# Weight parts stored with the columns of two neighbouring tiles by turns, and other start offsets for the activations

## Chip, cores and metric

The kernel runs on one core of one Trainium2 chip. The metric is the device time of one execution in microseconds (us); lower is better. The shapes are fixed: 256 positions, width 1024, two layers, feed-forward width 2816.

## What is computed

Both layers have the same frame, and the mixer in the middle differs: layer 0 has a convolution mixer, layer 1 attention.

```python
for layer in range(DEPTH):                                   # DEPTH = 2, SEQ = 256, D_MODEL = 1024
    x = x + 0.5 * swiglu_ffn(rms_norm(x, ffn1_norm[layer]), ffn1_w_gate_up[layer], ffn1_w_down[layer])
    h = rms_norm(x, mix_norm[layer])
    if layer % 2 == 0:
        x = x + conv_mixers(h, ...)          # projection 1024 -> 2560, two causal convolutions, projection back
    else:
        x = x + dilated_attention(h, ...)    # 16 heads of 64, projection 1024 -> 3072 and back
    x = x + 0.5 * swiglu_ffn(rms_norm(x, ffn2_norm[layer]), ffn2_w_gate_up[layer], ffn2_w_down[layer])
return rms_norm(x, final_norm)
```

Here `swiglu_ffn` is `(silu(x @ gate) * (x @ up)) @ w_down`, with 1024 to 2 x 2816 and back.

## The kernel before

The weights come as a stream of units. A unit is 128 partitions by 2048 float32: 16 tiles of 128 x 128, side by side, 1 MB, fetched by one DMA (`load`, into one of four buffers `raw`). Activations are held transposed, features on the partitions and the 256 positions along the row, so a weight tile is the stationary operand of a matmul and the activations are the moving operand.

Most units are split in two by `split(u)`: ScalarE copies `raw` to `w1` with rounding to the short type that TensorE takes in one pass (`F32R`, L127), and VectorE stores the rest, `w2 = raw - w1` (L128). Both work on halves of 1024 columns (some early units on quarters of 512). `w1` and `w2` have four buffers each, so a split waits until TensorE has finished with the unit four places earlier. Five units (`whole`) are not split and are multiplied as plain float32 (L161).

The activations are split in the same way into two parts, next to each other in the row: `xs` (inputs of a projection) and `gs` (the inner activations of a feed-forward). Three forms of product follow. `mm2` (L169, L170) multiplies `w1` with both activation parts in one matmul of 512 columns and then `w2` with the first part, 256 columns: this is "a pair" below. `mm3` (L163 to L165) does the same work as three matmuls of 256 columns, with `w1` loaded twice. For the values of the attention (L164 and so on with 512 columns) the roles are swapped: the activations are stationary and the weights are moving. Every matmul loads its stationary operand anew; the load of the next one runs while the present one streams.

The stages follow each other in time: in a feed-forward, 22 units of gate and up (`project2`, or `project` with `mm3` for a few of them), then 176 tiles of down (`mm2`, the last output tile with `mm3`). There are four feed-forwards, a convolution mixer between the first two and an attention between the last two. [...]

Where things lie in a row of the on-chip memory is set by hand. A first tile named "gap" fills up to a multiple of `LINE` = 1024 bytes, so that the weight buffers start on such a multiple; each weight tile is 512 bytes long. `XS_START` gives, for each norm and layer, how many bytes behind the start of its memory `xs` begins, and `GS_START` the same for `gs` of the four feed-forwards.

Of the kernel before, what the change touches and what calls it, by code (L numbers as in the profile page):

```python
# [10 lines left out]
F32 = mybir.dt.float32  # L11
# [6 lines left out]
P = 128  # L18
# [15 lines left out]
UT = 16  # L34
# [25 lines left out]
WIDEC = 0  # L60
LINE = 1024
BASE = 16512
XS_START = {"F1": (256, 32), "MX": (192, 256), "F2": (256, 32)}
GS_START = (800, 0, 800, 736)
GROUPS = ((0, 2), (2, 4), (4, 6), (6, 8))
M_POOL = [0, 0, 0, 0]
T_POOL = [0, 0, 0, 0]
# [27 lines left out]
def trunk(ctx: ExitStack, tc: tile.TileContext, xin, wst, cst, bia, idn, out):  # L95
    nc = tc.nc
# [12 lines left out]
    raw, w1, w2 = {}, {}, {}  # L109
# [8 lines left out]
    def split(u):  # L118
        if u in whole:
            return  # L120
        w1[u] = w1s.tile([P, UT * P], F32R, name="w1")
        w2[u] = w2s.tile([P, UT * P], F32R, name="w2")
        n = max(2, PIECES.get(u, 1), FINE.get(u - first_conv, 1))
        h = UT * P // n
        for i in range(n):
            c = slice(i * h, (i + 1) * h)
            nc.scalar.copy(w1[u][:, c], raw[u][:, c])  # L127
            nc.vector.tensor_sub(w2[u][:, c], raw[u][:, c], w1[u][:, c].bitcast(F32))  # L128
        del raw[u]

    def advance(u, ahead_split=ahead_split):
        while at["load"] < min(n_units, u + ahead_load):
            load(at["load"])
            at["load"] += 1
        while at["split"] < min(n_units, u + ahead_split):
            split(at["split"])
            at["split"] += 1


    first_conv = NF + NF * ND // UT  # L140
    whole = {0} | {first_conv + i for i in WHOLE} | {first_conv + 10, first_conv + 11}

    class Stream:
        def __init__(self, u):
# [2 lines left out]
        def tile(self, t, n=1):  # L147
            u, s = self.u + t // UT, t % UT
            c = slice(s * P, (s + n) * P)
            return (raw[u][:, c],) if u in whole else (w1[u][:, c], w2[u][:, c])  # L150

    used = [0]

    def take(n):
        st = Stream(used[0])
        used[0] += n
        return st
# [207 lines left out]
    def ffn(norm, after, between=None, first=None):  # L365
        _, r = norm.end(True, first is None)
        with tc.tile_pool(name="gp", bufs=1, reuse_waits="tile") as gp:
            st = take(NF)
            start = GS_START[st.u // FFN_STEP] // 4
            gs = gp.tile([P, NF * 2 * S + start], F32R, name="gs")[:, start:].rearrange(  # L370
# [339 lines left out]
    for lo, hi in START:  # L710
        c = slice(2 * lo * P, 2 * hi * P)
# [5 lines left out]
    for _ in range(WARM):  # L717
        nc.tensor.matmul(cold, ones, ones, start=True, stop=True)
    norm = Norm(C_F1, start=XS_START["F1"][0])
    for layer in range(DEPTH):  # L720
        nxt = Norm(C_MX + layer * ND, start=XS_START["MX"][layer])
        if layer == 0:
            ffn_first(norm, nxt)
        else:
            ffn(norm, nxt)
        norm, nxt = nxt, Norm(C_F2 + layer * ND, start=XS_START["F2"][layer])
        (conv if layer % 2 == 0 else attention)(norm, nxt)
        if layer < DEPTH - 1:
            norm, nxt = nxt, Norm(C_F1 + (layer + 1) * ND, start=XS_START["F1"][layer + 1])
            ffn(norm, nxt)  # L730
            norm = nxt
    with tc.tile_pool(name="fp", bufs=1, reuse_waits="tile") as fp:
# [6 lines left out]
        _, r = rsqrt_of([last.sums, last.sq], D, RMS_EPS, eps)  # L739
        for i, (lo, hi) in enumerate(GROUPS):  # L740
            n = hi - lo
# [93 lines left out]
```

## Time and profile before

| | |
|---|---|
| median of 3 runs | 969.8 us (968.5 to 969.87) |
| the profiled execution | 970.47 us, of which span 968.7 us |
| TensorE matmul / weight load busy | 953.3 us (98%) / 854.3 us (88%) |
| VectorE / ScalarE / GpSimd busy | 738.5 us (76%) / 557.8 us (58%) / 47.9 us (5%) |
| instructions; DMA | 15285; 176.27 MB, mean 182 GB/s |
| mean granted TensorE clock | 0.993 |

PE is TensorE's matmul row, PEld its weight loads, DVE is VectorE, ACT is ScalarE, POOL is GpSimd. A matmul's record is longer than its share of the time, because matmuls overlap in the pipeline. The pace, the distance from one start to the next, is therefore read from the first and the last start of a long row of equal instructions and their count. [...]

### The profile page before, as it was taken

To read this page: it belongs to the slowest core of one execution; us is meant where nothing else is said; L and a number is where in the kernel's file an instruction comes from. 1 tells how busy PE (TensorE), PEld (TensorE's weight loads), DVE (VectorE), ACT (ScalarE), POOL (GpSimd) and SP (SyncE) were. 2 spreads that over 40 slices of the span, in tenths; PEclk is the share of its full clock that TensorE was granted. 3 is DMA by queue.
4 is the path that set the end of the run, shared out by engine and by line. 5 is a ranking of instruction groups with operands and counts; after the bars stand their busy time and mean duration, and the time that the engine had idled before them with its cause. 6 is when DMAs were issued, how large, how long until landed. Compare 5 with 4: busy or idle time off the path is not lost.

```text
span 968.7 us, 15285 instructions
## 1 busy us (share of the span) xinstructions
PE 953.3 (98%) x5876; PEld 854.3 (88%) x5876; DVE 738.5 (76%) x1401; ACT 557.8 (58%) x1019; POOL 47.9 (5%) x61
## 2 busy tenths in 40 slices
PE   8999999999899999999999999999999999999996
PEld 8988898999798888988988889898888998889886
DVE  7977776688999878766787877666799798778552
ACT  6666554488366566544456565444677566565540
POOL 0000000039600000000000000000000000000000
PEclk9999999999899999999999999999999999999998
DMA  8855555444165555555455555555553455555501
GB/s 329 286 190 201 174 189 203 174 157 149 44 261 180 211 198 194 181 198 187 174 182 210 174 193 200 179 205 202 183 190 129 134 177 211 181 209 176 195 24 44
DMA packets 27289, 176.27 MB, mean 182 GB/s; under 512 B 3024, under 2 KB 3792, under 8 KB 6864
## 3 DMA queue, kind: packets, MB, share of 16 engines
q1 hardware_dynamic: 26784, 174.67, 51.7%
q8 instruction: 46, 0.75, 0.3%
q10 hardware_dynamic: 432, 0.63, 0.2%
q14 instruction: 27, 0.22, 0.1%
HBM read 174.23 MB, written 1.05 MB: 181 GB/s over the span
## 4 chain that ended last, share of the span: by engine, by line
PE 92%; DVE 3%; ACT 2%; POOL 1%; issue 1%; DMA 1%; SPq 0%; DVEq 0%; POOLq 0%; ACTq 0%
PE pa L169 33%; PE pa L170 17%; PE pb L169 15%; PE pb L170 8%; PE pa L165 4%; PE pa L163 4%; PE pa L164 4%; PE pa L161 2%; ACT prod L486 1%; DVE pb L464 1%; PE pb L164 1%; PE pb L163 1%; PE pb L165 1%; POOL yp L487 1%; DVE w L128 1%
## 5 line engine op out<-in xcount | busy, mean ns | idle before, releaser
L169 PE MATMUL pa<-xs,w 128*128 128x512 f32 x1376 | 480.8, 394 | 0.0
L128 DVE TENSOR_TENSOR w<-raw,w 128x1024 fp32r<-128x1024 f32 (+1 forms) x322 | 381.2, 1195 | 126.8 <-ACT w L127 126.1
L127 ACT CAST w<-raw 128x1024 fp32r<-128x1024 f32 (+1 forms) x322 | 325.0, 1027 | 132.5 <-PE pa L169 50.5
L170 PE MATMUL pa<-xs,w 128*128 128x256 f32 x1376 | 385.7, 280 | 0.0
L169 PEld LDWEIGHTS pa<-xs,w 128*128 128x128 f32 x1376 | 258.3, 188 | 58.0 <-DVE xs L191 0.5
L170 PEld LDWEIGHTS pa<-xs,w 128*128 128x128 f32 x1376 | 259.6, 189 | 0.1
L169 PE MATMUL pb<-gs,w 128*128 128x512 f32 x616 | 214.8, 392 | 0.0
L170 PE MATMUL pb<-gs,w 128*128 128x256 f32 x616 | 173.5, 282 | 0.0
L169 PEld LDWEIGHTS pb<-gs,w 128*128 128x128 f32 x616 | 115.7, 188 | 25.2
L170 PEld LDWEIGHTS pb<-gs,w 128*128 128x128 f32 x616 | 116.4, 189 | 0.0
L386 ACT ACTIVATE sl<-v 128x256 f32<-128x256 f32 x88 | 36.8, 419 | 106.3 <-DVE v L341 101.3
L339 ACT COPY sq<-pa 128x256 f32<-128x256 f32 x172 | 63.3, 369 | 30.4 <-PE pa L170 25.1
L164 PE MATMUL pa<-xs,w 128*128 128x256 f32 x272 | 76.5, 282 | 0.1
L163 PE MATMUL pa<-xs,w 128*128 128x256 f32 x272 | 76.5, 283 | 0.0
L165 PE MATMUL pa<-xs,w 128*128 128x256 f32 x272 | 76.4, 281 | 0.0
L340 DVE TENSOR_TENSOR v<-pa,sq 128x256 f32<-128x256 f32 x156 | 64.9, 416 | 0.0
L405 DVE SCALAR_TENSOR_TENSOR x<-pb,x 128x256 f32<-128x256 f32 x60 | 25.3, 422 | 43.0 <-PE pb L170 29.1
L487 POOL TENSOR_TENSOR yp<-yp,prod 128x256 f32<-128x256 f32 x55 | 46.2, 843 | 211.3 <-ACT prod L486 207.3
L190 ACT ACTIVATE xs<-x,const 128x256 fp32r<-128x256 f32 x48 | 24.2, 505 | 56.5 <-DVE x L405 43.2
L341 DVE TENSOR_TENSOR v<-v,rr 128x512 f32<-128x512 f32 x78 | 53.2, 683 | 0.0
L164 PEld LDWEIGHTS pa<-xs,w 128*128 128x128 f32 x272 | 51.8, 190 | 0.5 <-DVE xs L191 0.3
L165 PEld LDWEIGHTS pa<-xs,w 128*128 128x128 f32 x272 | 51.4, 189 | 0.4 <-DVE w L128 0.4
(176 smaller groups left out, 980.8 us busy)
## 6 DMA issues: line engine op xcount, KB each, us to landing
raw<-wst SPq DMA_DIRECT2D x159, 1024.0 KB, 4.8
bt<-bia SPq DMA_DIRECT2D x8, 384.0 KB, 3.3
raw<-wst SPq DMA_DIRECT2D x7, 256.0 KB, 6.3
raw<-wst SPq DMA_DIRECT2D x2, 512.0 KB, 5.6
x<-xin SPq DMA_DIRECT2D x3, 256.0 KB, 6.1
out<-y SPq DMA_DIRECT2D x2, 256.0 KB, 2.5
out<-y ACTq DMA_DIRECT2D x2, 256.0 KB, 2.4
x<-xin SPq DMA_DIRECT2D x2, 128.0 KB, 2.9
```

The source lines that it names most:

```text
L127: nc.scalar.copy(w1[u][:, c], raw[u][:, c])
L128: nc.vector.tensor_sub(w2[u][:, c], raw[u][:, c], w1[u][:, c].bitcast(F32))
L163: nc.tensor.matmul(o, a[0], b[0], start=start, stop=False, skip_group_check=check)
L164: nc.tensor.matmul(o, a[0], b[1], start=False, stop=False, skip_group_check=check)
L165: nc.tensor.matmul(o, a[1], b[0], start=False, stop=stop, skip_group_check=check)
L169: nc.tensor.matmul(o, w[0], b, start=start, stop=False, skip_group_check=True)
L170: nc.tensor.matmul(o[:, 0], w[1], b[:, 0], start=False, stop=stop, skip_group_check=True)
L339: nc.scalar.copy(h, bank[:, 1])
L340: nc.vector.tensor_add(v[:, i], bank[:, 0], h)
L341: nc.vector.tensor_mul(v, v, twice(r))
L386: nc.scalar.activation(sl, v[:, 0], AF.Silu)
L487: nc.gpsimd.tensor_add(yp[:, c], yp[:, c], t)
```

## The change

The two parts of a split unit are stored in another order. Two neighbouring tiles share 256 columns, and their columns alternate: column 0 of the even tile, column 0 of the odd tile, column 1 of the even tile, and so on. `split` reads `raw` as before and writes `w1` and `w2` with a step of two elements (8 bytes); VectorE reads `w1` back with that step. A stationary operand is then 128 elements with a step of two, over 1024 bytes instead of 512. The four units of attention values, whose weights are the moving operand, stay as they were (`plain`), and so do the five `whole` units. The number of instructions and of elements in each is unchanged.

Besides, `XS_START` and `GS_START` get other values: the two entries of the mixers stay, the other four of the first list change, and so do three of the four of the second.

```diff
-XS_START = {"F1": (256, 32), "MX": (192, 256), "F2": (256, 32)}
-GS_START = (800, 0, 800, 736)
+TWIN = 2
+XS_START = {"F1": (32, 128), "MX": (192, 256), "F2": (192, 64)}
+GS_START = (800, 896, 768, 864)
...
         n = max(2, PIECES.get(u, 1), FINE.get(u - first_conv, 1))
-        h = UT * P // n
+        h = UT // TWIN // n
+        r, o1, o2 = raw[u], w1[u], w2[u]
+        if u not in plain:
+            o1, o2 = woven(o1), woven(o2)
+            r = r.rearrange("p (b i c) -> p b i c", i=TWIN, c=P)
+        else:
+            h *= TWIN * P
         for i in range(n):
             c = slice(i * h, (i + 1) * h)
-            nc.scalar.copy(w1[u][:, c], raw[u][:, c])
-            nc.vector.tensor_sub(w2[u][:, c], raw[u][:, c], w1[u][:, c].bitcast(F32))
+            nc.scalar.copy(o1[:, c], r[:, c])
+            nc.vector.tensor_sub(o2[:, c], r[:, c], o1[:, c].bitcast(F32))
...
+    def woven(w):
+
+        return w.rearrange("p (b c i) -> p b i c", i=TWIN, c=P)
...
+    first_values = 3 * first_conv + 14
+    plain = set(range(first_values, first_values + 4))
...
-            return (raw[u][:, c],) if u in whole else (w1[u][:, c], w2[u][:, c])
+            if u in whole:
+                return (raw[u][:, c],)
+            if u in plain:
+                return w1[u][:, c], w2[u][:, c]
+            return tuple(woven(w)[:, s // TWIN, s % TWIN] for w in (w1[u], w2[u]))
```

## Rows read from the trace of the kernel before

**Rows 1.** Page, busy time of each engine, and engines of the chain that ended last.

```profile
PE 953.3 (98%) x5876; PEld 854.3 (88%) x5876; DVE 738.5 (76%) x1401; ACT 557.8 (58%) x1019; POOL 47.9 (5%) x61
...
PE 92%; DVE 3%; ACT 2%; POOL 1%; issue 1%; DMA 1%; SPq 0%; DVEq 0%; POOLq 0%; ACTq 0%
```

**Rows 2.** Longest waits of PE: us in total, times, longest us.

```profile
PE pa L161 <- DVE ya L539: 3.7, 1, 3.7
PE pa L353 <- DMA raw<-wst: 1.8, 1, 1.8
```

**Rows 3.** Busy time by stage: gate-up, down, convolution (second part), attention; columns as headed.

```profile
core 0: us, PE busy (x) PEld busy (x) DVE busy (x) ACT busy (x) POOL busy (x), PEclk, DMA share, GB/s
...
249.00:297.00 48.00, 44.29 (x247) 39.38 (x246) 44.01 (x111) 24.15 (x47) 9.57 (x13) 0.93 0.47 176
...
474.00:597.00 123.00, 123.00 (x726) 109.41 (x725) 100.48 (x176) 73.69 (x131) 0.00 (x0) 1.00 0.54 187
597.00:658.00 61.00, 61.00 (x376) 54.94 (x375) 38.37 (x54) 28.46 (x40) 0.00 (x0) 1.00 0.56 193
658.00:760.00 102.00, 101.89 (x646) 89.25 (x645) 82.04 (x240) 70.76 (x181) 0.00 (x0) 1.00 0.51 173
```

**Rows 4.** One line's matmuls, L170: count, min/median/max ns, first and last start us.

```profile
L170 PE MATMUL pa<-xs,w x171: 277/281/284, 59.7 to 119.8; 128*128 128x256 f32 x171
...
L170 PE MATMUL pa<-xs,w x174: 274/277/280, 309.8 to 369.8; 128*128 128x256 f32 x174
...
L170 PE MATMUL pb<-gs,w x151: 277/281/284, 413.0 to 466.0; 128*128 128x256 f32 x151
...
L170 PE MATMUL pb<-gs,w x145: 282/282/282, 600.0 to 649.9; 128*128 128x256 f32 x145
```

**Rows 5.** The same for L164, one of each three matmuls of `mm3`, four stretches.

```profile
L164 PE MATMUL pa<-xs,w x34: 283/283/283, 19.8 to 31.7; 128*128 128x256 f32 x34
...
L164 PE MATMUL pa<-xs,w x16: 276/276/367, 201.7 to 206.8; 128*128 128x256 f32 x16
...
L164 PE MATMUL pa<-xs,w x77: 281/281/281, 220.1 to 246.9; 128*128 128x256 f32 x77
...
L164 PE MATMUL pb<-gs,w x22: 277/279/280, 950.5 to 957.8; 128*128 128x256 f32 x22
```

**Rows 6.** Float32 units, L161: fifteen merged in the timeline (start, us), and one's durations.

```profile
208.81 3.40 PE L161 MATMUL pa<-xg,raw 128*128 128x256 f32 x15
...
L161 PE MATMUL pa<-xg,raw x64: 377/379/382, 207.7 to 255.3; 128*128 128x256 f32 x64
```

**Rows 7.** Groups by form, the two instructions of a split: busy us, mean ns, idle before.

```profile
L127 ACT CAST w<-raw 128x1024 fp32r<-128x1024 f32 x306 | 316.2, 1049 | 129.1 <-PE pa L169 50.5 <-issue 35.4 <-PE pb L169 24.0
...
L128 DVE TENSOR_TENSOR w<-raw,w 128x1024 fp32r<-128x1024 f32 x306 | 370.0, 1220 | 126.8 <-ACT w L127 126.1
```

**Rows 8.** Timeline of DVE over one gate-up unit: start, us, instruction, idle before.

```profile
520.11 1.22 DVE L128 TENSOR_TENSOR w<-raw,w 128x1024 fp32r<-128x1024 f32 x1 [1.01 <-ACT w L127]
...
521.92 1.21 DVE L128 TENSOR_TENSOR w<-raw,w 128x1024 fp32r<-128x1024 f32 x1
...
524.22 0.43 DVE L388 TENSOR_TENSOR g<-sl,v 128x256 f32<-128x256 f32 x1 [0.15 <-ACT sl L386]
525.66 1.22 DVE L128 TENSOR_TENSOR w<-raw,w 128x1024 fp32r<-128x1024 f32 x1 [1.01 <-ACT w L127]
```

**Rows 9.** Groups by form, two DVE operations of one kind on two SBUF inputs.

```profile
L191 DVE SCALAR_TENSOR_TENSOR xs<-x,const,xs 128x256 fp32r<-128x256 f32 x48 | 23.1, 481 | 12.3 <-ACT xs L190 12.3
...
L527 DVE SCALAR_TENSOR_TENSOR ya<-m,const,ya 128x256 f32<-128x256 f32 x8 | 5.4, 677 | 4.3 <-ACT ya L518 4.3
```

## The prediction

> **What bounds the kernel now.** First the busy shares and the chain that ended last [rows 1]: PE has 98% of the span and 92% of the chain, everything else together 8%. Then PE's waits [rows 2]: the two longest are 3.7 and 1.8 us, so PE is fed nearly all the time. Then the busy time by stage [rows 3]: PE is at 100% in gate-up, down and attention, and only the second part of the convolution shows DVE at 44.0 us of 48 with PE at 44.3. So the time is the number of matmuls times their pace, except in the convolution, where DVE and POOL set the speed and a quicker PE brings little.
>
> The pace is next. In two long stretches a pair (512 and 256 columns) starts every 347 ns: 49.9 us over 144 steps, and 60.0 over 173; in two others every 353 ns: 34.9 over 99 and 60.1 over 170 [rows 4]. The instructions are the same in all four, and the granted clock is 1.00. In the first gate-up stage `xs` begins at byte 256, in the second down stage `gs` begins at 0; these are the slow ones. Yet the stretch from 309.8 us also has `xs` at 256 and is a fast one, so the start sets what paces are possible and not alone which. The matmuls of `mm3` tell the same: a step of three takes 11.9 us over 33, 5.1 over 15, 26.8 over 76 and 7.3 over 21 [rows 5], that is 120, 113, 118 and 116 ns for each 256 columns.
>
> What would it cost without a disturbance? [...] The float32 matmuls of L161 show the fixed cost: fifteen fill 3.40 us with the last one's record of 379 ns [rows 6], so 14 steps take 3.02 us, 216 ns a step, with a weight load behind each. [...] A pair at that rate would take 325 ns, a matmul of 256 columns 109. The pairs lose 22 to 28 ns, the others 4 to 11.
>
> My reading is this. The loss depends on where the moving operand lies, so the two streams that TensorE reads, moving operand and next weights, meet in the memory. A float32 moving operand advances one column in 216/256 = 0.84 ns. A weight load of 128 columns fits in the 113 ns of rows 5's quickest stretch, so at most 0.88 ns a column; taking it to fill that time, it runs at the pace of the float32 operand, and these two, side by side, lose nothing. An `F32R` operand runs at 0.42 to 0.47 ns a column, twice as fast, so it passes the weights' addresses again and again. With a step of two the weights advance 8 bytes a column, as fast as that operand: the streams keep their distance, as in L161. This is inferred, as no row shows a step of two on any engine.
>
> **The change part by part.** *Stationary operands.* A pair goes from 346.7 to 325 ns (21.7 saved) or from 353.3 (28.3 saved). Counts by the loops: gate-up has 17, 21, 21 and 19 units with pairs, 16 each, of which 272 in the slow first stage and 976 elsewhere; down has 154 a stage, one stage slow; queries and keys have 128. Slow: (272 + 154) x 28.3 = 12.1 us. Fast: (976 + 462 + 128) x 21.7 = 34.0 us. Matmuls of 256 columns: 432 in gate-up, 264 in down, 288 in the two output projections. Those where `xs` or `gs` starts at 256 or 0, and the output projections, I put at 120 ns: 192 + 48 + 66 + 288 = 594 x 10.8 = 6.4 us. The other 390 x 7.5 = 2.9 us. The 384 of the convolution's input projection I count at nothing, since DVE hides them; if they counted, it would be 3.2 us. Sum 55.4 us.
>
> What is left over is unknown. The three mm3 paces of 113, 117 and 120 ns lie about 3.3 ns apart, which I take as the price of one meeting. Bounds for the 4968 counted matmuls: none keeps one (0) or each keeps one (16.5 us). I take a quarter, 4.1 us, near the low end, as L161 keeps none.
>
> *Start offsets.* Alone, they would bring the slow stages to the fast pace: 426 x 6.7 + (192 + 48 + 66) x 3.3 = 3.9 us. This lies within the sum above.
>
> *The split.* The instructions and their elements stay, 306 of 1024 columns on each engine [rows 7], but their writes, and one of DVE's reads, get a step of two. No row has such a step. Lower bound 0: nothing in a step saves work. Upper bound from the nearest row, however far: two operations of one kind on 256 columns take 481 and 677 ns [rows 9]; the slower one reads from a shifted place while POOL is busy. That is 0.77 ns a column, or 0.78 us for 1024. I take 0, since a step of 8 bytes is nearer to a dense row than to anything else the trace shows, and keep the upper end for a rival. What hides a smaller cost: in a gate-up unit of 5.55 us (520.11 to 525.66) DVE stands idle 1.01 + 0.15 = 1.16 us [rows 8]. A pace of 325 ns makes the unit 5.20 us, which leaves 0.81 us for two splits. DVE may thus lose 0.40 us on each before the gain shrinks, and 0.58 before the kernel gets slower. ACT has 123 - 74 = 49 us free in that gate-up stage [rows 3], and 0.78 x 44 = 34 us would fit.
>
> [...]
>
> **Rivals.** *A, the streams keep their distance:* 970.5 - 55.4 + 4.1 = 919.2 us in the profiled execution. The median is 0.7 below that execution, so 918.5, rounded 918; with the residue at its bounds and the convolution's 3.2 us, 911 to 931.
>
> *B, only part of the meetings goes,* as the weights may not advance exactly as fast as assumed. Half of 55 us is 28: 942, with 931 to 955 as its range. For it: the unexplained two paces at one start.
>
> *C, the step does nothing and only the offsets count:* 969.8 - 3.9 = 966. Against it: nothing direct.
>
> *D, no change at all.* [...] The trace speaks against it, with 347 against 353 ns for the same pairs at different places, unless something else than the weights causes that.
>
> *E, slower: DVE becomes the bound in gate-up.* At the upper end of 0.78 us for a split, a unit takes 5.55 - 1.16 + 1.56 = 5.95 us, 0.40 more than now, and 88 units give 35 us. The convolution, where DVE is already full, adds some 10 units x 2 x 0.78 = 16 us. Down, with DVE at 38.4 of 61 us [rows 3], has room for 22 x 0.78 = 17 us and still gains its 13 + 3 us, and the output projections 3. So 970 + 35 + 16 - 19 = 1002; it decides from 0.58 us more per split.
>
> [...]
>
> *F, slower: the weight loads suffer.* A load now spans twice as many bytes. If each stretch of bytes it touches meets the moving operand once, the loss above the floor doubles instead of vanishing: 970 + 55 + 3 = 1028. The place is PE, in every pair, and it shows as a pair pace above 353 ns.
>
> **How the numbers follow.** A 0.57, B 0.13, C 0.06, D 0.05, E 0.12, F 0.07. The forecast is A's 918. For 8 in 10 the range takes in A, B, C and D: 910 to 972, leaving out E, F and a little of A. About 0.2% (2 us) is what a measurement of this kernel can tell from no change. Faster: A, B and C, 0.76. Same: D, 0.05. Slower: E and F, 0.19.
>
> **What would show it.** A: L170 paces of 325 to 331 ns in every gate-up and down stage whatever the start, 109 to 113 ns for mm3, the same L127 and L128 means, and DVE's share in gate-up near 90%. B: paces of 332 to 342. C or D: 346 to 347 everywhere, or the old mixture. E: L128 well above 1.6 us and PE waiting in gate-up for DVE. F: paces above 353 with L128 unchanged. The second part of the convolution should stay near 48 us in all of them but E. My sum is wrong first of all if weights do not advance at half the pace of an `F32R` operand.

## The result and the profile after

The changed kernel takes 983.0 us (median of 4 runs, 982.8 to 984.2) against 969.6 for the kernel before: a ratio of 1.0143, with a 95% interval of 1.0125 to 1.0161. It is slower by 13 us (1.4%); the forecast was 918.

The profiled execution has a span of 981.1 us, 12.4 more than before. The page's busy times come first (columns as in [rows 1]).

```profile
PE 966.2 (98%) x5876; PEld 872.6 (89%) x5876; DVE 739.7 (75%) x1401; ACT 584.9 (60%) x1019; POOL 48.0 (5%) x61
```

Then the longest of PE's waits, as in [rows 2].

```profile
PE pa L179 <- DVE ya L557: 3.1, 1, 3.1
```

DVE's total has hardly moved (738.5 before), ACT's has grown by 27 us, and PE does not wait more than before. PE itself has 13 us more, and its weight loads 18 us more. So the loss lies in the pace of PE, and these rows, the counterparts of [rows 4] and [rows 5], show where. Each has the count and the first and last start of the 256-column matmul of the pairs (L188, before L170), in the order of the stages; the last row is one of three of `mm3` (L182, before L164) in the convolution.

```profile
L188 PE MATMUL pa<-xs,w x171: 283/283/283, 59.8 to 119.9; 128*128 128x256 f32 x171
...
L188 PE MATMUL pb<-gs,w x150: 283/283/283, 135.9 to 188.5; 128*128 128x256 f32 x150
...
L188 PE MATMUL pa<-xs,w x172: 278/281/281, 309.9 to 369.9; 128*128 128x256 f32 x172
...
L188 PE MATMUL pb<-gs,w x150: 280/280/281, 415.0 to 468.0; 128*128 128x256 f32 x150
...
L188 PE MATMUL pa<-xs,w x314: 280/280/281, 485.0 to 596.3; 128*128 128x256 f32 x157
...
L188 PE MATMUL pb<-gs,w x142: 278/281/281, 604.9 to 654.7; 128*128 128x256 f32 x142
...
L188 PE MATMUL pa<-xs,w x298: 282/282/282, 795.1 to 902.0; 128*128 128x256 f32 x149
...
L188 PE MATMUL pb<-gs,w x146: 279/279/283, 910.9 to 961.8; 128*128 128x256 f32 x146
...
L182 PE MATMUL pa<-xs,w x90: 283/283/283, 217.9 to 250.0; 128*128 128x256 f32 x90
```

Four stages of before are not among [rows 4]; these are the first down, third gate-up, fourth gate-up and fourth down stage.

```profile
L170 PE MATMUL pb<-gs,w x152: 282/282/282, 134.7 to 187.1; 128*128 128x256 f32 x152
...
L170 PE MATMUL pa<-xs,w x318: 282/282/282, 481.0 to 590.9; 128*128 128x256 f32 x159
...
L170 PE MATMUL pa<-xs,w x303: 279/282/282, 786.5 to 891.2; 128*128 128x256 f32 x152
...
L170 PE MATMUL pb<-gs,w x146: 282/282/282, 900.0 to 950.2; 128*128 128x256 f32 x146
```

The distance from the first to the last start, over the count less one, is the pace of a pair. The starts are given to 0.1 us, so a pace is good to about 1 ns.

| stage | pairs | before, ns | after, ns | more, us |
|---|---|---|---|---|
| first gate-up | 272 | 353 | 353 | 0 |
| first down | 154 | 347 | 353 | 0.9 |
| second gate-up | 336 | 347 | 351 | 1.3 |
| second down | 154 | 353 | 356 | 0.5 |
| third gate-up | 336 | 347 | 356 | 3.0 |
| third down | 154 | 347 | 353 | 0.9 |
| fourth gate-up | 304 | 347 | 360 | 4.0 |
| fourth down | 154 | 347 | 351 | 0.6 |

That is 11 of the 12.4 us. `mm3` pays too: in the convolution's input projection it went from 118 to 32.1/89/3 = 120 ns, about 1 us over its 384 matmuls. Against that stands the convolution's second part, which took 48.0 us before [rows 3] and 46.5 in this execution (columns as in [rows 3]):

```profile
251.60:298.10 46.50, 42.97 (x251) 38.05 (x250) 43.75 (x111) 25.40 (x48) 9.14 (x13) 1.00 0.50 181
```

Before, PE stood still there for 3.7 us, waiting for DVE [rows 2], and behind that wait the granted clock was 0.50 from 261 to 265 us. Here the wait was 3.1 us and the clock stayed at 1.00. The other three executions of the changed kernel have a mean clock of 0.994 or 0.995, near the 0.993 of before, so this belongs to the one execution and not, as far as is known, to the change.

No stage of pairs became faster. The paces spread from 351 to 360 ns, so the place may still count.

The weight loads tell what is new in them. First a stepped load of the kernel after (L187), then a load of the same kernel whose stationary operand stayed dense (the attention's values), each with min/median/max ns.

```profile
L187 PEld LDWEIGHTS pa<-xs,w x1376: 193/197/198, 32.2 to 902.7; 128*128 128x128 f32 x197
...
L182 PEld LDWEIGHTS pa<-w,xs x32: 187/188/192, 664.5 to 686.7; 128*128 128x128 f32 x32
```

197 ns for a load with the step, 188 without. Last the two instructions of a split, by form, as in [rows 7]: ScalarE's copy takes 1144 for 1049 ns, VectorE's subtraction 1223 for 1220.

```profile
L135 DVE TENSOR_TENSOR w<-raw,w 128x1024 fp32r<-128x1024 f32 x306 | 370.7, 1223 | 140.0 <-ACT w L134 139.8
...
L134 ACT CAST w<-raw 128x1024 fp32r<-128x1024 f32 x306 | 344.8, 1144 | 129.6 <-PE pa L187 52.3 <-issue 34.8 <-PE pb L187 23.7
```

### The profile page after: what moved, and what is told of

The parts are those of the page before. It is cut to its first block, busy times and chain, and to the rows that moved or that the text cites. A ratio compares the mean times of both kernels' runs of the same rounds, so it can differ in the third digit from the quotient of the medians.

```text
span 981.1 us, 15285 instructions
## 1 busy us (share of the span) xinstructions
PE 966.2 (98%) x5876; PEld 872.6 (89%) x5876; DVE 739.7 (75%) x1401; ACT 584.9 (60%) x1019; POOL 48.0 (5%) x61
## 4 chain that ended last, share of the span: by engine, by line
PE 90%; DVE 4%; ACT 3%; POOL 1%; issue 1%; DMA 1%; SPq 0%; POOLq 0%; DVEq 0%; ACTq 0%
PE pa L187 33%; PE pa L188 17%; PE pb L187 15%; PE pb L188 7%; PE pa L181 4%; PE pa L183 4%; PE pa L182 4%; ACT prod L504 2%; PE pa L179 1%; PE pb L182 1%; PE pb L181 1%; PE pb L183 1%; DVE pb L482 1%; DVE w L135 1%; POOL yp L505 1%; ACT w L134 1%
## 5 line engine op out<-in xcount | busy, mean ns | idle before, releaser
L187 PE MATMUL pa<-xs,w 128*128 128x512 f32 x1376 | 489.5, 399 | 0.0
L134 ACT CAST w<-raw 128x1024 fp32r<-128x1024 f32 (+1 forms) x322 | 354.2, 1120 | 133.2 <-PE pa L187 52.3
L188 PE MATMUL pa<-xs,w 128*128 128x256 f32 x1376 | 386.6, 281 | 0.0
L187 PEld LDWEIGHTS pa<-xs,w 128*128 128x128 f32 x1376 | 270.5, 197 | 54.0 <-DVE xs L209 0.6
L188 PEld LDWEIGHTS pa<-xs,w 128*128 128x128 f32 x1376 | 270.7, 197 | 0.1
L187 PE MATMUL pb<-gs,w 128*128 128x512 f32 x616 | 217.8, 398 | 0.0
L188 PE MATMUL pb<-gs,w 128*128 128x256 f32 x616 | 173.0, 281 | 0.0
L187 PEld LDWEIGHTS pb<-gs,w 128*128 128x128 f32 x616 | 120.9, 196 | 23.6
L188 PEld LDWEIGHTS pb<-gs,w 128*128 128x128 f32 x616 | 121.1, 197 | 0.0
L182 PE MATMUL pa<-xs,w 128*128 128x256 f32 x272 | 77.2, 284 | 0.1
L183 PEld LDWEIGHTS pa<-xs,w 128*128 128x128 f32 x272 | 53.2, 195 | 0.4 <-DVE w L135 0.2
L182 PEld LDWEIGHTS pa<-xs,w 128*128 128x128 f32 x272 | 53.0, 195 | 0.4 <-DVE xs L209 0.3
```

The costliest lines, as they stand in the source:

```text
L134: nc.scalar.copy(o1[:, c], r[:, c])
L182: nc.tensor.matmul(o, a[0], b[1], start=False, stop=False, skip_group_check=check)
L183: nc.tensor.matmul(o, a[1], b[0], start=False, stop=stop, skip_group_check=check)
L187: nc.tensor.matmul(o, w[0], b, start=start, stop=False, skip_group_check=True)
L188: nc.tensor.matmul(o[:, 0], w[1], b[:, 0], start=False, stop=stop, skip_group_check=True)
```

## The experiments

Four suspects stood after this: the step in TensorE's reading, the step in the writes (ScalarE is slower by 27 us in all, and its stores could disturb TensorE), the new offsets, and a sum of them.

### Step alone

The changed kernel with the offsets of before:

```diff
-XS_START = {"F1": (32, 128), "MX": (192, 256), "F2": (192, 64)}
-GS_START = (800, 896, 768, 864)
+XS_START = {"F1": (256, 32), "MX": (192, 256), "F2": (256, 32)}
+GS_START = (800, 0, 800, 736)
```

> The step of two as in the change, but all start offsets as before. If the stationary operand's step is the cause, most of the 13 us stay: 978 to 986 us, with pair paces above 350 ns in the stages that had 347 before. If the new offsets are the cause, the time falls back to 968 to 972 us with the old paces. ScalarE's split copy should be 1144 ns as in the changed kernel either way.

Measured: 980.75 us, ratio 1.0121 (1.0106 to 1.0136). The step is the larger part. Two rows of L188, at starts that ran at 347 ns before (32 in the third gate-up, 800 in the third down):

```profile
L188 PE MATMUL pa<-xs,w x312: 283/283/283, 484.8 to 594.7; 128*128 128x256 f32 x156
...
L188 PE MATMUL pb<-gs,w x142: 283/283/283, 605.0 to 654.8; 128*128 128x256 f32 x142
```

109.9/311 and 49.8/141 are both 353 ns. At the offsets of before, the step brings every feed-forward stage to 353 ns, the longer of the two old paces, and leaves the stages that had it where they were.

### Offsets alone

The kernel before with the new offsets (the same two lines, the other way round).

> The new start offsets with the old dense layout. If the offsets are the cause, about 980 us. If the step is the cause: 966 to 972 us; places 32, 128, 192, 64 and 800, 896, 768, 864 then show which offset gives which pace with dense weights, those at 0 modulo 128 (128, 896, 768) the slow 353 ns and the others 347.

Measured: 973.2 us, ratio 1.0038 (1.0025 to 1.0051): slower, not the 966 to 972 expected. 32, 864 and 800 gave 347 ns. 128, 896 and 768 were slow as foreseen (351 to 353), but so were 192 and 64, which are 64 modulo 128. The rows of L170, first gate-up (`xs` at 32) and second (192), show 60.0/173 = 347 and 60.1/170 = 353 ns:

```profile
L170 PE MATMUL pa<-xs,w x174: 282/282/282, 59.8 to 119.8; 128*128 128x256 f32 x174
...
L170 PE MATMUL pa<-xs,w x171: 281/281/281, 309.7 to 369.8; 128*128 128x256 f32 x171
```

So with the dense layout the starts at 32 and 96 modulo 128 gave 347 ns here, those at 0 and 64 gave 351 to 353, and the new list has more of the latter than the old. It is no strict rule: the second gate-up stage of the kernel before ran at 347 ns with `xs` at 256.

### Stepped writes, dense reads

```diff
-            return tuple(woven(w)[:, s // TWIN, s % TWIN] for w in (w1[u], w2[u]))
+            return w1[u][:, c], w2[u][:, c]
```

> Old offsets; the split writes with the step of two, but TensorE reads its stationary operands dense, so the weights are in the wrong places and the values differ from the reference. If TensorE's own reading is the cause, 968 to 971 us and the old paces. If ScalarE's longer copy (1144 for 1049 ns) or its stepped writes disturb TensorE, 975 to 985 us.

Measured: 970.7 us, ratio 1.0015 (1.0005 to 1.0024). ScalarE's copy takes 1138 ns, nearly as long as in the changed kernel, and it costs little. Whether even the 1.6 us are its own is open, since two stages changed their pace at the old start: the second gate-up, with `xs` at 256, went from 347 to 60.0/170 = 353 ns, which is 336 x 6 = 2 us more, and the second down, with `gs` at 0, from 353 to 53.1/153 = 347, which is 1 us less. The fast stages stayed fast. The rows are those of the second gate-up, second down and third down:

```profile
L188 PE MATMUL pa<-xs,w x171: 277/281/284, 309.8 to 369.8; 128*128 128x256 f32 x171
...
L188 PE MATMUL pb<-gs,w x154: 278/280/280, 413.0 to 466.1; 128*128 128x256 f32 x154
...
L188 PE MATMUL pb<-gs,w x131: 282/282/282, 605.0 to 650.1; 128*128 128x256 f32 x131
```

### Dense writes, stepped reads

```diff
-        if u not in plain:
-            o1, o2 = woven(o1), woven(o2)
-            r = r.rearrange("p (b i c) -> p b i c", i=TWIN, c=P)
-        else:
-            h *= TWIN * P
+        h *= TWIN * P
```

> Old offsets; the split writes dense, but TensorE reads its stationary operands with the step of two, so the values differ from the reference. If TensorE's own reading is the cause, the same time as with the step alone (978 to 986 us), with weight load records of 197 for 189 ns. If the writes are the cause, 968 to 971 us.

Measured: 979.4 us, ratio 1.0104 (1.0089 to 1.0119); the copy is back at 1050 ns and the load at 197. The three stand against each other: reading 10.3 us, writing 1.6, both together (the step alone) 11.6. TensorE's reading is the cause of what the step loses.

### The moving operand held still

The forecast rested on two streams that meet. Here one of them stands still (dense layout, old offsets):

```diff
+    def still(b):
+        if len(b.shape) == 3:
+            return b[:, :1, :1].to_broadcast(list(b.shape))
+        return b[:, :1].to_broadcast(list(b.shape))
...
+        b = still(b)
         nc.tensor.matmul(o, w[0], b, start=start, stop=False, skip_group_check=True)
```

and the same in `mm3`, but for the float32 units. This run and the others whose results are given without a ratio were executed once each; the kernel before spread over 968.4 to 971.3 us beside them.

> Kernel before, dense weights and old offsets, but in mm2 and mm3 every moving operand is its first column repeated (a step of 0), so the products are left out but for one column. If the time above the floor comes from two streams meeting in the memory, the pairs fall from 347 and 353 ns to 325 ns, the rest from 117 and 120 to 109, and the whole to about 915 us. If it belongs to the weight load alone or is a fixed price of a change of weights, the paces stay.

Measured: 925.9 us. The pairs run at 60.0/182 = 330 ns in every stage, `mm3` at 24.2/72/3 = 112:

```profile
L178 PE MATMUL pa<-xs,w x183: 275/275/275, 309.9 to 369.9; 128*128 128x256 f32 x183
...
L171 PE MATMUL pa<-xs,w x73: 275/275/275, 207.8 to 232.0; 128*128 128x256 f32 x73
```

So 17 ns of a pair (23 in the slow stages), and all dependence on the place, come only when the moving operand makes its way through the memory; 5 ns above the assumed floor of 325 stay.

### The stationary operand held still

```diff
+    def still(w):
+        return w[:, :1].to_broadcast(list(w.shape))
...
+        w = [still(i) for i in w]
         nc.tensor.matmul(o, w[0], b, start=start, stop=False, skip_group_check=True)
```

> Kernel before, but in mm2 and mm3 the stationary operand is its first column repeated (a step of 0), so all output rows hold the same product. If two streams meet, again 325 and 109 ns. If the cost is in the moving operand's own reading, the paces stay at 347 and 353. If it is the number of places that a weight load touches, this run is at the floor and the moving one is not.

Measured: 964.4 us, 5 to 6 us less than the kernel before. The second gate-up stage stays at 59.9/172 = 348 ns, the slow first gate-up stage falls from 353 to the same 348, and `mm3` goes to 29.9/88/3 = 113:

```profile
L176 PE MATMUL pa<-xs,w x173: 274/279/281, 60.0 to 119.9; 128*128 128x256 f32 x173
...
L176 PE MATMUL pa<-xs,w x173: 274/279/281, 309.9 to 369.8; 128*128 128x256 f32 x173
...
L169 PE MATMUL pa<-xs,w x89: 275/276/277, 213.1 to 243.0; 128*128 128x256 f32 x89
```

This lies between the expectations. In the feed-forward every pair is at 347 or 348 ns, so the two streams together do make the 6 ns between a slow and a fast stage, and 3 to 7 ns of an `mm3` matmul in most stretches. But the pairs keep some 22 ns above the assumed floor of 325 without any way of the weights. That a load sweeps beside the moving operand is thus not what these 22 ns are made of, and no step of the weights could have given them back.

### A step of four, and the float32 units with a step of two

Dense writes as above, with

```diff
-    def woven(w):
+    def woven(w, n=4):
-        return w.rearrange("p (b c i) -> p b i c", i=TWIN, c=P)
+        return w.rearrange("p (b c i) -> p b i c", i=n, c=P)
...
-                return (raw[u][:, c],)
+                return (woven(raw[u], 2)[:, s // 2, s % 2],)
...
-            return tuple(woven(w)[:, s // TWIN, s % TWIN] for w in (w1[u], w2[u]))
+            return tuple(woven(w)[:, s // 4, s % 4] for w in (w1[u], w2[u]))
```

> Dense writes, old offsets; TensorE reads its split stationary operands with a step of four (16 bytes) and those of the float32 units with a step of two, so values differ from the reference. If a load costs by the stretches it touches, the pairs rise well above the 353 ns of the step of two, to 370 ns or more. If the step only decides how the two streams lie, they stay near 353. For the float32 units: if they are quiet because both streams go at one pace, the step of two lifts L161's counterpart above its 216 ns a matmul; if not, 216 stays.

Measured: 1358 us. The rows are L184 of the pairs with its load, and L178 of `mm3`.

```profile
L184 PE MATMUL pa<-xs,w x256: 282/284/284, 450.0 to 569.8; 128*128 128x256 f32 x128
...
L184 PEld LDWEIGHTS pa<-xs,w x256: 334/336/338, 449.7 to 569.6; 128*128 128x128 f32 x128
...
L178 PE MATMUL pa<-xs,w x83: 397/397/398, 309.8 to 367.8; 128*128 128x256 f32 x83
```

The timeline of the same kernel has 32 float32 matmuls merged in one row (start, us):

```profile
297.86 7.07 PE L175 MATMUL pa<-xg,raw 128*128 128x256 f32 x32
```

A pair with the step of four takes 119.8/255 = 470 ns and a matmul of `mm3` 58.0/82/3 = 236. A pair, with two loads, takes as long as two matmuls of `mm3`, with one load each, though one of its matmuls streams 512 columns. So the load has become the bound, at about twice the 117 ns that a matmul of `mm3` took before. By its record the load went from 188 to 336 ns; with a step of two it had grown by 9 ns, to 197.

The float32 matmuls take (7.07 - 0.379)/31 = 216 ns with a step of two, as in [rows 6] without. Their quiet pace does not hang on two operands that advance equally fast.

### Both held still

> Kernel before with moving and stationary operand of mm2 and mm3 both a repeated first column, so nearly all of the products are left out. The moving operand alone held still gave 330 and 111.7 ns. If the 5 and 2.7 ns that stay above 325 and 109 come from the weights' own sweep, this run shows 325 and 109; if they are a fixed price of an F32R matmul, 330 and 111.7 again.

The two edits above together. Measured: 926.4 us, pairs at 59.8/181 = 330 ns, `mm3` at 112:

```profile
L178 PE MATMUL pa<-xs,w x182: 275/275/275, 310.0 to 369.8; 128*128 128x256 f32 x182
```

The dense weights' sweep costs nothing beside a still moving operand; 330 and 112 are what these matmuls cost in this kernel even then.

### The step with the moving operand held still

> Step of two in TensorE's reading (dense writes, old offsets, other values) and the moving operand held still, so most products are left out. If the step's 6.7 ns a pair are paid only where a sweeping moving operand meets the load, the paces are 330 and 111.7 ns, as without the step, and the time some 926 us. If the step makes the load itself longer, they stand above: 336 and 115 ns or more, over 935 us.

Stepped reads with dense writes, and the moving operand's first column repeated. Measured: 941.7 us. L192 of the pairs, L185 of `mm3`, and the latter's load:

```profile
L192 PE MATMUL pa<-xs,w x179: 275/275/276, 309.9 to 369.8; 128*128 128x256 f32 x179
...
L185 PE MATMUL pa<-xs,w x80: 281/281/281, 211.9 to 239.8; 128*128 128x256 f32 x80
...
L185 PEld LDWEIGHTS pa<-xs,w x80: 196/196/196, 211.8 to 239.7; 128*128 128x128 f32 x80
```

59.9/178 = 337 and 27.9/79/3 = 118 ns: 7 and 6 more than without the step. The step makes the load itself longer, with no sweeping operand to meet. A pair with its two stepped loads pays about as much as one matmul of `mm3` with one.

### The step in one part only

A pair's first part streams 512 columns and its second 256. The second part's load runs behind the 512, the next first part's behind the 256, as the timeline of the kernel before shows (start and length in us):

```profile
340.10 0.39 PE L169 MATMUL pa<-xs,w 128*128 128x512 f32 x1
340.10 0.19 PEld L170 LDWEIGHTS pa<-xs,w 128*128 128x128 f32 x1
340.33 0.27 PE L170 MATMUL pa<-xs,w 128*128 128x256 f32 x1
340.33 0.19 PEld L169 LDWEIGHTS pa<-xs,w 128*128 128x128 f32 x1
```

If a load some 7 ns longer shows only behind the short one, the second part's step is free.

```diff
+            return w1[u][:, c], woven(w2[u])[:, s // TWIN, s % TWIN]
```

> Dense writes, old offsets; only the second weight part is read with the step of two, the first dense, so values differ from the reference. If each stepped load pays its own price, the pairs of the stages that had 346.7 ns go half way, to 350 ns, and the whole to some 975 us. If one stepped load is enough to put a pair into the slow pattern, 353 ns and 979 us; if only the load behind the 256 columns counts (the first part's), 347 ns and 970 us.

Measured: 965.5 us. All pairs of the feed-forward ran at 346 to 347 ns (59.9/173 and 60.0/173 in the first two gate-up stages, both at start 256):

```profile
L184 PE MATMUL pa<-xs,w x174: 278/278/278, 60.0 to 119.9; 128*128 128x256 f32 x174
...
L184 PE MATMUL pa<-xs,w x174: 281/281/281, 310.0 to 370.0; 128*128 128x256 f32 x174
```

None of the three expectations has this whole: the pace was the third one's, but the stages that had been slow became fast too, and the time fell below the 970 us named there.

The other way round:

```diff
+            return woven(w1[u])[:, s // TWIN, s % TWIN], w2[u][:, c]
```

> Dense writes, old offsets; only the first weight part is read with the step of two, so values differ from the reference. If a stepped load is longer by some 7 ns and shows only where it runs behind 256 columns, all pairs are at 353.3 ns (their first part's load runs behind the 256 columns), as with both parts stepped, and the whole at 978 to 980 us; mm3 pays on two of three loads, about 119 ns or the 120 of both. If it is the number of stepped loads that counts, the pairs are at 347 ns as with the second part alone, and the whole near 966 us.

Measured: 975.5 us. The pairs ran at 59.9/171 = 350 (first gate-up), 60.0/170 = 353 (second) and 47.4/135 = 351 ns (third down):

```profile
L184 PE MATMUL pa<-xs,w x172: 278/280/282, 60.0 to 119.9; 128*128 128x256 f32 x172
...
L184 PE MATMUL pa<-xs,w x171: 278/278/278, 309.9 to 369.9; 128*128 128x256 f32 x171
...
L184 PE MATMUL pb<-gs,w x136: 276/278/280, 604.8 to 652.2; 128*128 128x256 f32 x136
```

Against the 347 ns of the run with the second part's step, the first part's costs the pairs 3 to 6 ns, and the second part's costs none. Against dense weights the two stages that had been fast lose 4 to 6 ns, while the first gate-up went from 353 to 350. The size is a little below what was expected (350 to 353 for 353.3, and 975.5 for 978 to 980 us), and the 353 of both parts is not the sum of the two. So it is shown that the first part's load is the one that pays; that it pays because it runs behind the shorter stream is argued, and these rests are not explained.

### Better places

Dense layout, `xs` at 32 and `gs` at 800 throughout:

> Kernel before, dense, with xs at 32 in every stage and gs at 800 in every stage, the places that ran at 346.7 ns. All pairs at 346.7 and all mm3 of xs and gs at 116.7 ns: 426 x 6.7 and 306 x 3.3 ns less, and a little in the attention, so 964 to 967 us. If the place does not decide the pace, 968 to 971 us.

Measured: 966.5 us, ratio 0.9967 (0.9955 to 0.9978). All pairs at 347 ns but those of the fourth down stage (350); the attention's values, where `xs` is the stationary operand, went from 227 to 233 ns a matmul (the records from 389 to 396). With these two put back to where they were (`xs` 256 in the attention, `gs` 736 in the fourth feed-forward):

> Dense layout; xs at 32 but at 256 in the attention, gs at 800, 800, 800 and 736. Against all at 32 and 800, the 96 matmuls of the attention's values go from 233 back to 227 ns and the last down stage from 350.1 to 346.7 ns: 0.6 + 0.5 us less, so 964 to 967 us.

Measured: 965.7 us, ratio 0.9950 (0.9933 to 0.9967). And with 32 bytes ahead of the operands of the two output projections:

```diff
+            cp.tile([P, 8], F32, name="gap3")
             ob = [cp.tile([P, 4, S], F32R, name=f"ob{i}") for i in range(2)]
...
+            ap.tile([P, 8], F32, name="gap4")
             o1 = ap.tile([P, 8, S], F32R, name="o1")
```

> The best places so far, and before the operands of the two output projections a gap of 32 bytes. If their 120 ns came from the place (0 modulo 128), they go to 116.7 ns, and the whole falls by 288 x 3.3 = 1.0 us to 963 to 966 us. If not, 964 to 967 us with 120 ns as before.

Measured: 965.2 us, ratio 0.9957 (0.9940 to 0.9973). Against the run before it the time tells nothing, but the records of the projections' matmuls (L164) did go from 283 to 280 ns. At 965 us, with the weights dense, this kernel is 4 us faster than the one before and 18 us faster than the changed one.

## Why the prediction was wrong

**What held.** PE bounds the kernel and its pace is the time. The splits stay hidden: VectorE's subtraction did not change (value 0 taken, 3 ns measured: 1223 for 1024 columns against 1220 dense), and ScalarE's 95 ns more per copy cost little, no more than the 1.6 us of the run with stepped writes and dense reads. So rival E did not come. The second part of the convolution did not become slower.

**The step that failed** is the one marked as inferred: that weights with a step of two would keep their distance to the moving operand, "as in L161". Three parts of it fell. L161's counterpart keeps its 216 ns with a step of two, so equal speed was not the reason for its pace. With the stationary operand held still, the pairs still take 348 ns and the whole kernel 964.4 us, so two sweeps passing each other make 5 to 6 us in all (the 353 of the slow stages and part of `mm3`) and not 55; the rest of the loss appears with the moving operand's own sweep (330 ns without it). And no run shows the 325 ns of a pair and the 109 of 256 columns that the sum counts down to: `F32R` matmuls took 330 and 112 with both operands still, so there 256 columns more cost 330 - 2 x 112 = 106 ns. So most of the term of 46.1 us for the pairs was not to be had by any layout of the weights. Of the 9.3 us for `mm3` a part was there (113 ns with the weights held still), but the step gave none of it back: 120 ns.

**The price that was missing.** The sum held no cost for the stepped load. That a stepped load takes no longer than a dense one was the author's assumption; the records show 197 against 188 ns. The step costs some 7 ns, 337 against 330 ns a pair and 118 against 112 for `mm3`, and in the real kernel it moves stages from 347 to 353 ns. Rival F had the direction, the engine and the sign by which to know it (paces above 353 in the fourth gate-up, L128's counterpart unchanged), with 0.07. Its reason was not needed, as the load is longer also where it meets nothing, and its price of 1028 us was too high by 45, since it let the whole loss above the floor double. What does double, between a step of two and one of four, is the load: from 120 to 236 ns a matmul of `mm3`.

**The offsets** were counted as a gain of 3.9 us within the sum. Alone they cost some 4 us (973.2 against 969.1 for the kernel before beside it), because the term took every new start for a fast one: 128, 896 and 768 are 0 modulo 128, like the known slow starts, and 192 and 64 proved slow too. That rival C would have given 966 was wrong for the same reason. Rival D, no change at all, did not come either. Where the moving operand stands still, the way of dense weights costs nothing: 330 ns a pair whether they sweep or not. Where it sweeps, it costs a little in some stages: holding the weights still took the slow pairs from 353 to 348 ns and `mm3` from 117 and 120 to 113. And a load with a step of four, 336 ns by its record, set a pace of 236 ns a matmul.

**A reading that was wrong.** The 384 matmuls of the convolution's input projection were put at nothing, as hidden behind DVE. Only the convolution's second part is bound that way. In the stretch before it PE was full (columns as in [rows 3]), and these matmuls count:

```profile
195.00:249.00 54.00, 53.66 (x428) 52.32 (x426) 47.08 (x110) 44.89 (x92) 38.08 (x44) 1.00 0.38 132
```

**Open.** Why the same start (256 or 0) runs at 347 ns in one stage or kernel and at 353 in another. Why a stepped second part brings such stages to 347, and why stages at 353 pay nothing for the step in both parts. Why the new offsets together with the step reach 356 and 360 ns, which neither reaches alone. And what in the moving operand's sweep costs the 17 ns: its own reading of ever new places, or other engines and the DMA that work in the same memory beside it, or the values, which are all alike in a repeated column. No run separates these.

## What to carry to other kernels

Before a loss is given to two streams that meet, hold each of them still in a run of its own: a repeated first column is a small edit, and it would have shown here that the weights' way holds 5 to 6 us and not 55. Where a matmul is short, its time may be that of a weight load, and anything that lengthens the load can show at once, as in `mm3` (118 for 112 ns with the moving operand still); in the pairs the step of the second part, whose load runs behind 512 columns, cost nothing (346 to 347 ns). An analogy between two rows that differ in more than one thing, as float32 and `F32R` matmuls do, gives a rival and not a forecast.

## What the runs showed of the hardware

A weight load with a step of 8 bytes takes 197 for 188 ns by its record, one with 16 bytes 336; in pace, `mm3` goes from 117 or 118 ns dense over 120 to 236. With dense weights, a moving operand of 4-byte elements that starts at 32 or 96 modulo 128 bytes gave 347 ns a pair (350 in one stage of one run), one at 0 or 64 mostly 351 to 353. A moving operand that does not advance gives 330 (and 112 for 256 columns in `mm3`), and a stationary one that does not advance 347 to 348 at every start. A float32 matmul of 256 columns takes 216 ns, an `F32R` one of `mm3` with dense weights 113 to 120. ScalarE's copy of 1024 columns takes 1049 ns to a dense place and 1138 to 1144 to one with a step of 8 bytes, VectorE's subtraction 1220 and 1223.
